# A hybrid decoder block on one core: GpSimd makes the RWKV stage's weight halves

## The chip, the cores and the metric

The kernel runs on one core of one Trainium2 chip. A core has five engines with a queue each, and each queue runs in order: TensorE (PE in the profile; its weight loads are listed apart as PEld), VectorE (DVE), ScalarE (ACT), GpSimd (POOL) and SyncE (SP), which here only issues DMAs. The metric is the device time of one execution in microseconds, lower is better; a time is given as the median of several runs.

## The reference

One decoder block over 512 tokens with a model width of 2048, batch 1, all in float32. What is computed, cut to its frame:

```python
c_act = silu(c)
mod = c_act @ w_ada + b_ada                     # six vectors: shift, scale, gate, twice
h = rmsnorm(x, norm1_g) * (1 + sc1) + sh1
p = h @ w_in                                    # 2048 -> 4384 columns
y_rwkv = rwkv7(p[..., :3360], ...)              # 16 heads of 64, state recurrence over 512 steps
y_pool = causal_pool(p[..., 3360:], ...)        # windows 2, 4, 8, 16
x = x + gt1 * (concat(y_rwkv, y_pool) @ w_out)
h = rmsnorm(x, norm2_g) * (1 + sc2) + sh2
x = x + gt2 * conv_ffn(h, w_up, conv_w, w_down) # 2048 -> 2 x 5632 -> 2048
out = rmsnorm(x, norm_f_g)
```

The projections need more precision than one pass of TensorE's rounded float type gives, so each is made of three products (below).

## The kernel before

**A projection.** Tokens lie along the free dimension (512 of them), features along the 128 partitions. Each activation tile is kept as two tiles, a rounded copy (hi) and the remainder (lo). Weights come in chunks of 128x512 floats (256 KB), that is four 128x128 blocks. `split_weights` loads a chunk into `wraw` (a DMA on SP's queue, four buffers), makes the rounded copy `whi` on ScalarE (L105, three buffers) and the remainder `wlo = wraw - whi` on VectorE (L107, three buffers). `mm3` then multiplies hi by hi (L111), hi by lo (L112) and lo by hi (L113) into one PSUM tile. One chunk feeds 12 matmuls, and `project` walks the chunks of one output tile. A `whi` buffer is free again when the last matmul on L112 of its chunk has run, a `wlo` buffer after the last on L113, and a `wraw` buffer when L107 has read it.

**The stages.** (1) Modulation vectors, the first norm, and the first eight tiles of the input projection (`pf`). (2) The RWKV stage, to which the change belongs: eight pairs of heads pass through `stage_a` (decay, keys, a small triangular solve on VectorE with trips through DRAM), `stage_b` (growing the inverse from 32 to 64 and 128 wide) and `stage_c` (four chunks of the recurrence, then a group norm). Among them stand the other 27 tiles of the input projection, made by `win_tile` into the PSUM tiles `mm` (two buffers): `win_pair` makes three for each of the pairs 1 to 7, and the last loop six more for the pooling groups. So 27 x 4 = 108 chunks are split in this stage. `ada_rest` (L334 and L336) works out the other modulation vectors on VectorE at the same time, 192 loads `war` and 192 dot products `jkr`. (3) The output projection, the second norm, the up projection with its convolution, and the down projection (`b` tiles), which fill the rest of the time.

**What sets the order.** The program is traced into a list, and the tile framework lays out ahead of time one fixed order for each engine: by priority, by what is ready in a plan that it makes with its own costs, and by which buffers are free. `hp()` puts the pairs' own work ahead of everything; the projection tiles and `ada_rest` fill in between. On the chip each engine follows its fixed order and waits at semaphores, so an instruction that waits holds up all that is behind it on its engine. Moving work to another engine makes the framework lay out all the orders anew.

**What else stands on the engines.** ScalarE has the activations of the pairs, with table loads, and the copies out of PSUM. VectorE has the masks, the triangular solve, the scans and `jkr`. GpSimd runs nothing but thirteen memsets, the last of them on L318 before the first pair. `project` and `split_weights` are also called in the stages (1) and (3).

Of the kernel before, what the change touches and what calls it, by code (L numbers as in the profile page):

```python
# [9 lines left out]
F32 = mybir.dt.float32  # L10
# [3 lines left out]
ALU = mybir.AluOpType  # L14
PSUM = bass.MemoryType.PSUM

P = 128
# [6 lines left out]
WC = 512  # L24
# [29 lines left out]
def block_kernel(ctx, tc, a, out, stop=None, dbg=None):  # L54
    nc = tc.nc
    V, S, G, PE = nc.vector, nc.scalar, nc.gpsimd, nc.tensor
# [41 lines left out]
    b1p = cp.tile([P, KT], F32, tag="b1p", name="b1p")  # L98
    V.tensor_scalar_add(b1p, cols("b_ada", 16, 32), 1.0)

    def split_weights(src):
        raw = wp.tile([P, WC], F32, tag="wraw", name="wraw", bufs=4)
        nc.sync.dma_start(raw, src)
        hi = wp.tile([P, WC], F32R, tag="whi", name="whi", bufs=3)
        S.copy(hi, raw)  # L105
        lo = wp.tile([P, WC], F32R, tag="wlo", name="wlo", bufs=3)
        V.tensor_tensor(lo, raw, hi[:, :].bitcast(F32), op=ALU.subtract)  # L107
        return hi, lo

    def mm3(ps, wh, wl, xh, xl, start, stop):  # L110
        PE.matmul(ps, wh, xh, start=start, stop=False)  # L111
        PE.matmul(ps, wh, xl, start=False, stop=False)  # L112
        PE.matmul(ps, wl, xh, start=False, stop=stop)  # L113

    def project(ps, src, acts, start=True, stop=True):

        n = len(acts)
        for k0 in range(0, n, WC // P):
            wh, wl = split_weights(src[:, k0 * P : k0 * P + WC])
            for kk in range(WC // P):  # L120
                k = k0 + kk
                sl = slice(kk * P, (kk + 1) * P)
                mm3(ps, wh[:, sl], wl[:, sl], *acts[k], start=start and k == 0, stop=stop and k == n - 1)

    def slots(k, tag="a"):
        return (actp.tile([P, T], F32R, tag=f"{tag}h{k}", name=f"{tag}h{k}"),
                actp.tile([P, T], F32R, tag=f"{tag}l{k}", name=f"{tag}l{k}"))
# [39 lines left out]
    if True:  # L167
# [27 lines left out]
        H = []  # L195
        for k in range(KT):
            for part in (1, 0):
                j = part * 16 + k
                wa = p0.tile([P, D], F32, tag="wa", name="wa", bufs=4)
                nc.sync.dma_start(wa, a["ada1"][j, :, :])  # L200
                jk = p0.tile([P, D], BF16, tag="jk", name="jk", bufs=1)
                V.scalar_tensor_tensor(jk, wa, 1.0, cb, op0=ALU.mult, op1=ALU.mult,
                                       accum_out=mod[:, j : j + 1])
            V.scalar_tensor_tensor(gsc1[:, k : k + 1], mod[:, 16 + k : 17 + k], b1p[:, k : k + 1],
                                   col("n1", k), op0=ALU.add, op1=ALU.mult)
            V.tensor_add(mod[:, k : k + 1], mod[:, k : k + 1], col("b_ada", k))
            h = p0.tile([P, T], F32, tag="h", name="h", bufs=2)
            hi, lo = slots(k)
            modulate(hi[:, :], lo[:, :], h, xs[k], rstd, gsc1[:, k : k + 1], mod[:, k : k + 1])
            H.append((hi, lo))  # L210
            for i0 in range(0, 8, WC // P):
                wh, wl = split_weights(a["win0"][k, :, i0 * P : i0 * P + WC])
                for ii in range(WC // P):
                    sl = slice(ii * P, (ii + 1) * P)
                    mm3(pf[i0 + ii], wh[:, sl], wl[:, sl], *H[k], start=k == 0, stop=k == KT - 1)
# [79 lines left out]
    def mmtile():  # L295
        return psa.tile([P, T], F32, tag="mm", name="mm", bufs=2)
# [9 lines left out]

    def win_tile(fi):
        ps = mmtile()
        project(ps, a["win1"][fi - 8, :, :], H)
        return ps  # L310

    sbd = [ra.tile([P, P], F32, tag=f"sbd{i}", name=f"sbd{i}") for i in range(2)]
# [278 lines left out]
    def win_pair(p):  # L591
        for i in range(3):
            ps = win_tile(8 + 3 * (p - 1) + i)
            t = ra.tile([P, T], F32, tag="spill", name="spill", bufs=2)
            shift(ps, 8 * i + p, t)
            d = tc.dram_tile([P, T], F32, name=f"sp{p}_{i}")
            nc.sync.dma_start(d, t)
            sp[p, i] = d
# [33 lines left out]
    for n, gi in enumerate((1, 2, 0)):  # L632
        upad = []
        for i in range(2):
            ps = win_tile(29 + 2 * n + i)
            u = ring16("upad")
            V.memset(u[:, 0:16], 0.0)
            S.copy(u[:, 16:], ps)
            upad.append(u)
        with hp():  # L640
            pool_group(gi)
# [17 lines left out]
    def bank():  # L659
        return psm.tile([P, T], F32, tag="b", name="b")  # L660
# [44 lines left out]
    def up_first(hf, k):  # L705
        hs = slice(hf * HT, (hf + 1) * HT)
        wh, wl = split_weights(a["wup0"][k, :, :])
        for i in range(4):
            sl = slice(i * P, (i + 1) * P)
            mm3(ups[i][:, hs], wh[:, sl], wl[:, sl], H2[k][0][:, hs], H2[k][1][:, hs], start=k == 0, stop=k == KT - 1)  # L710
# [4 lines left out]
    for k0 in range(0, KT, 4):  # L715
        for f in range(KT):
            project(pss[f], a["wout"][f, :, k0 * P : (k0 + 4) * P], mh[k0 : k0 + 4],
                    start=k0 == 0 and f % 2 == 0, stop=k0 == KT - 4 and f % 2 == 1)
        if k0 == 4:
            x2 = []  # L720
            for f in range(KT):
                t = rb.tile([P, T], F32, tag=f"x2_{f}", name=f"x2_{f}")
                nc.sync.dma_start(t, a["xT"][:, f, :])
                x2.append(t)
# [5 lines left out]
    for f in range(KT):  # L730
        if f == NORM_AT:
            dg = norm_rows(acc0)
        if f == NORM_AT + 1:
            rstd = norm_bcast(dg)
        if NORM_AT + 1 <= f < NORM_AT + 9:
            second_norm(0, rstd, 2 * (f - NORM_AT - 1))
            second_norm(0, rstd, 2 * (f - NORM_AT - 1) + 1)
        ps = bank()[:, 0:HT]
        project(ps, a["wout"][f, :, :], mh)
        acc1 = residual(1, f, ps, acc1)  # L740
# [49 lines left out]
    for gi, gn in enumerate(GROUPS):  # L790
# [17 lines left out]
        if gi < len(GROUPS) - 1:  # L808
            for f in range(KT):
                ps = bank()  # L810
# [131 lines left out]
```

## Time and profile before

| | us |
|---|---|
| median of 3 runs | 2465.12 (2463.72 to 2469.42) |
| the profiled execution's own time | 2465.06 |
| its span, from the first instruction to the last | 2463.3 |
| PE busy | 2355.7 (96%) |
| VectorE busy | 1450.8 (59%) |
| ScalarE busy | 912.6 (37%) |
| GpSimd busy | 2.7 |

The profile's times count from the start of the span. "Busy" for PE is the time covered by at least one matmul; matmuls overlap, so the time of one is read from the distance between two starts. In the table of waits a line says which instruction waited, for which, and how long its engine sat idle in total. In a group's line, the figure behind the bar's second stroke is the idle time of the engine just before these instructions, and what ended it. The RWKV stage lies between about 155 us and 800 us.

### The profile page before, as it was taken

How to read it: one execution, taken by the hardware profiler on the slowest of the kernel's cores; microseconds unless marked ns; L12 is line 12 of the kernel's file. 1: busy time of each engine (PE TensorE's matmuls, PEld its weight loads, DVE VectorE, ACT ScalarE, POOL GpSimd, SP SyncE). 2: the span in 40 equal slices, each digit the busy share in tenths (PEclk: the TensorE clock that was granted, in tenths of full speed). 3: DMA queues.
4: the chain of work that ended last, by engine and by line, in shares of the span. 5: the costliest groups of instructions: out<-in, count | busy, mean ns of one | idle time of the engine just before them, and what ended most of it. 6: DMA issues, size and time to landing. Idle time of an engine off the chain costs nothing.

```text
span 2463.3 us, 37835 instructions
## 1 busy us (share of the span) xinstructions
PE 2355.7 (96%) x14386; PEld 1907.4 (77%) x14386; DVE 1450.8 (59%) x2804; ACT 912.6 (37%) x1476; POOL 2.7 (0%) x13
## 2 busy tenths in 40 slices
PE   4889999999998999999999999999999999999997
PEld 3656666666665999887788888888888888888897
DVE  7987777787774477747634443444344433544467
ACT  3244443444334456533223322333233322323354
POOL 0000000000000000000000000000000000000000
PEclk9999999999999999999999999999999999999999
DMA  9965565566554755537532233223322232322255
GB/s 361 338 222 150 164 184 159 145 182 177 169 167 137 237 183 184 181 103 253 182 97 96 98 95 98 98 96 99 95 98 99 95 99 96 97 98 95 98 156 187
DMA packets 240232, 367.40 MB, mean 149 GB/s; under 512 B 75761, under 2 KB 81073, under 8 KB 235825
## 3 DMA queue, kind: packets, MB, share of 16 engines
q1 hardware_dynamic: 240050, 364.99, 46.8%
q8 instruction: 112, 1.84, 0.3%
q14 instruction: 70, 0.57, 0.1%
HBM read 348.90 MB, written 16.00 MB: 148 GB/s over the span
## 4 chain that ended last, share of the span: by engine, by line
PE 68%; DVE 3%; DMA 2%; ACT 1%; issue 1%; SPq 0%; DVEq 0%; ACTq 0%
PE b L113 21%; PE b L111 21%; PE b L112 21%; DMA slot<-ada 1%; DVE slot L774 1%; PE pa L283 1%; PE mm L111 1%; PE mm L112 1%; PE mm L113 1%; DVE wlo L107 0%; DMA wraw<-wup 0%; DMA war<-ada 0%; DMA mxl<-mixd 0%; DVE x L825 0%; PE pb L522 0%
## 5 line engine op out<-in xcount | busy, mean ns | idle before, releaser
L107 DVE TENSOR_TENSOR wlo<-wraw,whi 128x512 fp32r<-128x512 f32 x844 | 579.8, 689 | 694.6 <-ACT whi L105 681.9
L105 ACT CAST whi<-wraw 128x512 fp32r<-128x512 f32 x844 | 524.1, 622 | 1215.4 <-PE b L112 950.2
L113 PE MATMUL b<-hh,wlo 128*128 128x512 f32 (+1 forms) x1472 | 557.6, 381 | 9.7 <-DVE wlo L107 9.6
L111 PE MATMUL b<-hh,whi 128*128 128x512 f32 (+1 forms) x1472 | 559.2, 380 | 0.0
L112 PE MATMUL b<-hl,whi 128*128 128x512 f32 (+1 forms) x1472 | 558.6, 380 | 0.0
L111 PE MATMUL b<-ah,whi 128*128 128x256 f32 (+1 forms) x1344 | 442.2, 329 | 1.4 <-ACT mxp L286 0.9
L112 PE MATMUL b<-al,whi 128*128 128x256 f32 (+1 forms) x1344 | 441.3, 329 | 0.0
L113 PE MATMUL b<-ah,wlo 128*128 128x256 f32 (+1 forms) x1344 | 441.2, 329 | 0.0
L113 PEld LDWEIGHTS b<-hh,wlo 128*128 128x128 f32 x1472 | 275.6, 188 | 65.8 <-DVE wlo L107 13.3
L111 PEld LDWEIGHTS b<-hh,whi 128*128 128x128 f32 x1472 | 277.2, 188 | 53.1 <-ACT whi L105 0.5
L112 PEld LDWEIGHTS b<-hl,whi 128*128 128x128 f32 x1472 | 277.2, 188 | 52.0
L111 PEld LDWEIGHTS b<-ah,whi 128*128 128x128 f32 x1344 | 255.3, 190 | 26.9 <-ACT ah L131 2.4
L112 PEld LDWEIGHTS b<-al,whi 128*128 128x128 f32 x1344 | 255.5, 190 | 23.5 <-DVE al L132 1.0
L113 PEld LDWEIGHTS b<-ah,wlo 128*128 128x128 f32 x1344 | 255.4, 190 | 22.1 <-DVE wlo L107 0.2
L111 PE MATMUL mm<-ah,whi 128*128 128x512 f32 x432 | 179.1, 415 | 5.0 <-ACT upad L255 5.0
L112 PE MATMUL mm<-al,whi 128*128 128x512 f32 x432 | 178.4, 413 | 0.0
L113 PE MATMUL mm<-ah,wlo 128*128 128x512 f32 x432 | 177.3, 410 | 0.0
L336 DVE SCALAR_TENSOR_TENSOR jkr<-war,cq 128x512 bf16<-128x512 f32 x192 | 131.4, 684 | 20.9 <-DMA war<-ada 19.1
L812 DVE SCALAR_TENSOR_TENSOR x<-b,mod,x 128x512 f32<-128x512 f32 x80 | 59.7, 751 | 110.8 <-PE b L113 110.8
L111 PEld LDWEIGHTS mm<-ah,whi 128*128 128x128 f32 x432 | 82.0, 190 | 32.1 <-issue 10.2
L112 PEld LDWEIGHTS mm<-al,whi 128*128 128x128 f32 x432 | 82.1, 190 | 27.8 <-issue 12.7
L113 PEld LDWEIGHTS mm<-ah,wlo 128*128 128x128 f32 x432 | 82.1, 190 | 22.9 <-issue 6.9
(230 smaller groups left out, 2099.3 us busy)
## 6 DMA issues: line engine op xcount, KB each, us to landing
wraw<-wup SPq DMA_DIRECT2D x368, 256.0 KB, 3.0
wraw<-wdn SPq DMA_DIRECT2D x208, 256.0 KB, 2.7
war<-ada SPq DMA_DIRECT2D x192, 256.0 KB, 3.5
wraw<-win SPq DMA_DIRECT2D x140, 256.0 KB, 4.0
wa<-ada SPq DMA_DIRECT2D x32, 1024.0 KB, 7.1
wraw<-wout SPq DMA_DIRECT2D x128, 256.0 KB, 3.4
slot<-ada SPq DMA_DIRECT2D x64, 256.0 KB, 3.9
sp<-spill SPq DMA_DIRECT2D x21, 256.0 KB, 2.7
```

Source lines behind the costliest of these rows:

```text
L105: S.copy(hi, raw)
L107: V.tensor_tensor(lo, raw, hi[:, :].bitcast(F32), op=ALU.subtract)
L111: PE.matmul(ps, wh, xh, start=start, stop=False)
L112: PE.matmul(ps, wh, xl, start=False, stop=False)
L113: PE.matmul(ps, wl, xh, start=False, stop=stop)
L283: PE.matmul(ps, pw[:, i, d * P : (d + 1) * P], zs[i], start=i == 0, stop=i == 1)
L336: V.scalar_tensor_tensor(jk, wa, 1.0, cq[0], op0=ALU.mult, op1=ALU.mult, accum_out=modq[:, kq, j : j + 1])
L774: V.scalar_tensor_tensor(jk, wa, 1.0, cbs[kq], op0=ALU.mult, op1=ALU.mult, accum_out=modg[:, kq, j : j + 1])
L812: V.scalar_tensor_tensor(x2[f], ps, mod[:, 80 + f : 81 + f], x2[f], op0=ALU.mult, op1=ALU.add)
```

## The change

`split_weights` and `project` take a flag, and `win_tile` sets it: in the RWKV stage both halves of a chunk are made by GpSimd, the rounded copy with `tensor_copy` and the remainder with `tensor_tensor`. The DMA of the chunk, the buffers and the matmuls stay as they are in the code, and the other calls of `project` keep ScalarE and VectorE.

```diff
-    def split_weights(src):
+    def split_weights(src, pool=False):
         raw = wp.tile([P, WC], F32, tag="wraw", name="wraw", bufs=4)
         nc.sync.dma_start(raw, src)
         hi = wp.tile([P, WC], F32R, tag="whi", name="whi", bufs=3)
-        S.copy(hi, raw)
         lo = wp.tile([P, WC], F32R, tag="wlo", name="wlo", bufs=3)
-        V.tensor_tensor(lo, raw, hi[:, :].bitcast(F32), op=ALU.subtract)
+        if pool:
+            G.tensor_copy(hi, raw)
+            G.tensor_tensor(lo, raw, hi[:, :].bitcast(F32), op=ALU.subtract)
+        else:
+            S.copy(hi, raw)
+            V.tensor_tensor(lo, raw, hi[:, :].bitcast(F32), op=ALU.subtract)
         return hi, lo
...
-    def project(ps, src, acts, start=True, stop=True):
+    def project(ps, src, acts, start=True, stop=True, pool=False):
...
-            wh, wl = split_weights(src[:, k0 * P : k0 * P + WC])
+            wh, wl = split_weights(src[:, k0 * P : k0 * P + WC], pool)
...
     def win_tile(fi):
         ps = mmtile()
-        project(ps, a["win1"][fi - 8, :, :], H)
+        project(ps, a["win1"][fi - 8, :, :], H, pool=True)
         return ps
```

## The prediction

> **What bounds the kernel now.** I read the page's shares first, then the busy times of the RWKV stage alone, then who waited for whom in it.
>
> ```profile
> span 2463.3 us, 37835 instructions
> PE 2355.7 (96%) x14386; PEld 1907.4 (77%) x14386; DVE 1450.8 (59%) x2804; ACT 912.6 (37%) x1476; POOL 2.7 (0%) x13
> ```
>
> ```profile
> core 0: us, PE busy (x) PEld busy (x) DVE busy (x) ACT busy (x) POOL busy (x), PEclk, DMA share, GB/s
> 155.00:800.00 645.00, 613.55 (x5524) 421.40 (x5523) 469.30 (x1203) 274.44 (x422) 0.00 (x0) 0.98 0.56 165
> ```
>
> TensorE has matmuls in flight in 613.6 of the stage's 645 us. So 31.4 us of idle is all that a better flow on the other engines can win here, save the small stalls that overlapping matmuls cover. VectorE is busy 73% of the stage, ScalarE 43%, GpSimd not at all. The waits of PE in this stretch:
>
> ```profile
> PE pa L283 <- DMA pw<-poolw: 6.7, 1, 6.7
> PE mm L111 <- ACT upad L255: 5.0, 1, 5.0
> PE pa L402 <- DVE bt L394: 4.1, 2, 2.2
> PE ch L584 <- ACT rs L578: 3.5, 6, 0.9
> PE pb L455 <- DMA x<-dxz: 3.2, 3, 1.4
> PE pb L477 <- DVE xy L469: 3.0, 4, 1.9
> PE pb L465 <- issue: 1.1, 1, 1.1
> PE pa L360 <- DMA lw<-lora: 0.9, 2, 0.5
> PE pb L484 <- DVE Tm L479: 0.8, 1, 0.8
> PE pb L496 <- DVE x L488: 0.8, 2, 0.5
> PE ch L532 <- DVE L L524: 0.5, 2, 0.3
> PE pa L442 <- DVE nt L405: 0.4, 1, 0.4
> PE pb L501 <- ACT Tm L498: 0.2, 1, 0.2
> PE ch L576 <- ACT sqy L574: 0.2, 1, 0.2
> ```
>
> Neither `whi` nor `wlo` is among them: weights are not late today. The first two (11.7 us) stand at the ends of the stage: the PSUM of the `pf` tiles, which ScalarE must first copy out, and the last pooling group's weights. Of the rest, VectorE and ScalarE end 4.1 + 3.5 + 3.0 + 0.8 + 0.8 + 0.5 + 0.4 + 0.2 + 0.2 = 13.5 us, all work of the pairs.
>
> **What the change removes.** The groups of the stage by shape:
>
> ```profile
> L336 DVE SCALAR_TENSOR_TENSOR jkr<-war,cq 128x512 bf16<-128x512 f32 x192 | 131.4, 684 | 20.9 <-DMA war<-ada 19.1 <-DMA cq<-cact 0.4
> L107 DVE TENSOR_TENSOR wlo<-wraw,whi 128x512 fp32r<-128x512 f32 x110 | 75.3, 687 | 53.0 <-ACT whi L105 48.2 <-PE mm L113 2.3 <-PE mm L112 2.0
> L105 ACT CAST whi<-wraw 128x512 fp32r<-128x512 f32 x110 | 67.9, 619 | 153.3 <-PE mm L112 112.5 <-DMA wraw<-win 12.3 <-DVE jkr L336 6.4
> ```
>
> Of the 110 of each, 108 move (27 tiles of 4 chunks; the other two are neighbouring stages'). That takes 108 x 0.687 = 74 us off VectorE and 108 x 0.619 = 67 us off ScalarE. It also takes away waits that block a queue: ScalarE stood 153 us before the casts, mostly for a buffer that PE frees, with the pairs' work behind it, and VectorE 53 us for the cast. Where this reaches a pair, the chain of waits shows it:
>
> ```profile
> 677.98 0.62 ACT whi L105
> ...
> 678.61 1.28 ACT L578
> ```
>
> The cast is run just before the group norm's table load and logarithm on L578, for which L584 waits.
>
> What is it worth? None of the 13.5 us is a wait for the moved instructions themselves; it is a wait for pair work that shares an engine with them. The most it can give is the 13.5 us, the least nothing. The moved work with its waits is 75.3 + 53.0 of VectorE's 645 us and 67.9 + 153.3 of ScalarE's, 20% and 34%. If a stall shrank by the share of its engine, that would be about a quarter of 13.5; a cast that blocks just at the end of a chain, as above, counts for more. Between the two ends I take somewhat under half: 6 us.
>
> **What it adds.** No instruction of GpSimd in this trace reads anything. Its nearest rows are memsets:
>
> ```profile
> 0.73 0.53 POOL L72 MEMSET scanm<- 128x516 f32 x1 [0.29 <-POOLq L931]
> ...
> 149.93 0.96 POOL L316 MEMSET xy<- 128x1024 f32 x1
> ```
>
> That is about 0.5 us for one stream of 512 floats per partition. The copy has two streams: 0.5 us if they overlap, 1.0 if not. The subtraction has three: 0.5 to 1.6. So a chunk costs 1.0 to 2.6 us, against 0.62 + 0.69 = 1.31 on the two engines now. I take 2.1, the copy overlapped, the subtraction not, since the memsets show only that one stream is no slower than on VectorE. 108 x 2.1 = 227 us, 35% of the stage, on an engine that has nothing else; behind a GpSimd instruction that waits for a `whi` buffer there are only later chunks. [...]
>
> **Why that is hidden.** What PE needs is a chunk in time. The densest run of `mm` matmuls, and the casts in it:
>
> ```profile
> 684.70:703.70 19.00, 18.31 (x81) 14.83 (x79) 0.00 (x0) 1.16 (x2) 1.00 0.81 215
> ```
>
> ```profile
> 684.68 0.62 ACT L105 CAST whi<-wraw 128x512 fp32r<-128x512 f32 x1 [0.56 <-PE mm L112]
> 687.41 0.62 ACT L105 CAST whi<-wraw 128x512 fp32r<-128x512 f32 x1 [2.11 <-PE mm L112]
> ...
> 698.29 0.62 ACT L105 CAST whi<-wraw 128x512 fp32r<-128x512 f32 x1 [2.10 <-PE mm L112]
> 701.01 0.62 ACT L105 CAST whi<-wraw 128x512 fp32r<-128x512 f32 x1 [2.10 <-PE mm L112]
> ```
>
> One chunk each 2.72 us, for about seven chunks (81 of 84 matmuls), each cast waiting for the buffer that PE frees. Three chunks stand ready when a run begins. If GpSimd takes S per chunk, the seventh is ready about 2.3 + 4S after the start (the first release, then four chunks) and is needed by L113 at 6 x 2.72 + 0.45 = 16.8. So S may be 3.6 us before PE waits at all, and over the stage a chunk is used only each 645 / 108 = 6.0 us. At 2.1, and at 2.6, the late weights cost nothing. If that cover is gone (S over 3.6), it is the third rival.
>
> The queue in front moves little. SP issues `wraw` when the remainder has been read out of the old chunk:
>
> ```profile
> SPq L103 <- DVE wlo L107: 116.2, 40, 18.4
> ```
>
> Behind such a wait stand `war` loads, for which VectorE idled 19.1 us (row of L336). A release later by 2.1 - 1.31 = 0.8 us in 40 waits is 32 us of SP's time at most; in that proportion VectorE would lose 19.1 x 32 / 116 = 5 us more. That is a twelfth of what it is freed of, and I count it with the gain's discount. The buffers' number and the DMAs stay; the order of every engine is laid out anew, which can pack PE's queue better or worse by some microseconds either way.
>
> **The sum.** 2465.1 (the profiled execution, 0.06 us from the median of the runs) - 6 + 0 = 2459 us. A difference under 0.2%, 4.9 us, is about what a measurement of this kernel can't tell from none.
>
> **The rivals.**
>
> *First: no change, 2465.* The stage is 95% filled with matmuls; a wait that ends earlier on one engine may only be followed by the next (the DMA of `x`, 3.2 us, stands right behind the solve on VectorE). For it: the small size of all waits, and that no single one has the moved work as its releaser. Against it: the cast in the chain above.
>
> *Second: GpSimd holds VectorE up, slower, 2483.* While GpSimd reads its operands, a VectorE instruction with two operands in SBUF could have to wait for the whole of it, and the pairs' work on VectorE would come late. GpSimd is in the way for up to 227 us, and VectorE is freed of 75.3 + 53.0 = 128 us. The rival decides from the point where 128 / 227 = 56% of GpSimd's time falls on waiting VectorE instructions. At three quarters VectorE loses 170 - 128 = 42 us net, 5.3 in each of eight pairs. Projection matmuls that today run after the last pair can be pulled forward to fill PE's time:
>
> ```profile
> 759.00:787.00 28.00, 23.99 (x104) 1.00 0.54 168
> ```
>
> That is 24 us, 3.0 per pair, and leaves 2.3 x 8 = 18 us: 2483. For it: L336 (131 us) and the moved subtraction's neighbours read two SBUF tiles. Against it: the masks and copies of the recurrence read one of theirs from PSUM, and there PE takes few projection chunks.
>
> ```profile
> L524 DVE TENSOR_TENSOR L<-pb,masks 128x384 f32<-128x384 f32 x64 | 34.4, 554 | 15.7 <-PE pb L522 15.2
> L541 DVE COPY U<-ch 128x128 f32<-128x128 f32 x32 | 9.3, 290 | 21.9 <-PE ch L539 17.3 <-ACT R L535 3.6 <-ACT whi L105 0.6
> ```
>
> [...]
>
> *Third: chunks come late, 2476.* With 2.1 us and a VectorE instruction of 0.69 in front of each half, S is 3.5, just under 3.6. With 2.6 it is 4.0: (4.0 - 3.6) x 4 = 1.6 us in each of some seven dense runs, 11 us.
>
> *Fourth: a much better packing, 2448.* All 13.5 us go, and the small stalls that the matmuls' overlap hides, some 4 us more.
>
> **How the numbers follow.** The forecast has 0.40, with 2452 to 2464 as its own range; the first rival 0.27, the second 0.15, the third 0.10, the fourth 0.08. Below 2460.2 (faster) lie three quarters of the forecast and the fourth rival, 0.30 + 0.08, and 0.01 of the first: 0.39. Within 0.2% lie the forecast's rest and nearly all of the first: 0.10 + 0.25 = 0.35. Slower are the second, the third and 0.01 of the first: 0.26. The range, 2446 to 2484, holds the forecast, the first, third and fourth and the smaller half of the second; the least and greatest gain (0 and 13.5 with hidden stalls) and the dear end of a chunk (2.6 with VectorE in front) lie in it.
>
> **What would show it.** Right: GpSimd 200 to 240 us busy in the stage, a chunk near 2 us from start to start; VectorE and ScalarE some 70 us less busy each, and PE's waits for `bt`, `rs` and `xy` down by some 6 us; none on the new `whi` or `wlo`. The second rival: the mean of L336 or of the two-SBUF operations well over 0.69 us, or gaps before them that GpSimd ends, and more PE waits for `bt` and `xy`. The third: PE waits for `wlo` in dense runs. Wrong in any case: a shift outside 155 to 800 us, since nothing there is edited.

## The result, and the profile after

The changed kernel takes 2505.26 us (median of 4 runs, 2500.37 to 2512.29), the kernel before, run beside it, 2467.27 (2463.72 to 2470.67). The ratio is 1.0158, with a 95% interval of 1.0136 to 1.018: 38 us slower, where 2459 was forecast and the range ended at 2484. The profiled execution took 2505.43 us.

In the code after, the lines from `split_weights` on stand a few lower: L107 and L108 are GpSimd's copy and subtraction, L110 and L111 those that ScalarE and VectorE keep for the other stages; the matmuls of a chunk are L115 to L117, and everything later is 4 lower (L336 is L340, L586 is L590). In kernels of the experiments the lines move by a few more.

The page of the changed kernel, its span and shares, and then the RWKV stage alone (its end has moved from 800 to 838 us; columns as in the prediction):

```profile
span 2503.7 us, 37893 instructions
PE 2364.6 (94%) x14386; PEld 1912.3 (76%) x14386; DVE 1459.4 (58%) x2696; ACT 849.8 (34%) x1368; POOL 240.2 (10%) x229
```

```profile
155.00:838.00 683.00, 621.60 (x5530) 427.00 (x5529) 476.85 (x1098) 213.03 (x314) 234.46 (x214) 0.97 0.54 156
```

The stage is 38 us longer, so nearly the whole loss lies in it (the two profiled executions are 40.4 us apart). TensorE is idle for 683 - 621.6 = 61.4 us, twice the 31.4 of before, and covers 8 us more although it has the same matmuls. ScalarE lost 61 us of work, of the 67 forecast. VectorE did not get lighter: 108 subtractions are gone, and yet it is busy 476.9 us against 469.3. That is the line to stop at. The groups of the changed kernel on VectorE and GpSimd in the stage (busy us, mean ns of one, then idle before them), beside the one row of before that the prediction doesn't show:

```profile
L340 DVE SCALAR_TENSOR_TENSOR jkr<-war,cq 128x512 bf16<-128x512 f32 x192 | 146.4, 762 | 27.1 <-DMA war<-ada 23.7 <-DMA cq<-cact 1.6
L528 DVE TENSOR_TENSOR L<-pb,masks 128x384 f32<-128x384 f32 x64 | 34.4, 553 | 14.1 <-PE pb L526 13.2
L424 DVE TENSOR_TENSOR prod<-xyl,nl 64x14 f32<-64x14 f32 (+6 forms) x112 | 33.8, 302 | 1.5
L545 DVE COPY U<-ch 128x128 f32<-128x128 f32 x32 | 9.3, 289 | 25.4 <-PE ch L543 19.8 <-ACT R L539 4.3 <-PE pa L406 1.1
L108 POOL TENSOR_TENSOR wlo<-wraw,whi 128x512 fp32r<-128x512 f32 x107 | 155.7, 1455 | 25.2 <-PE mm L117 17.7
L107 POOL CAST whi<-wraw 128x512 fp32r<-128x512 f32 x107 | 79.7, 745 | 406.4 <-PE mm L116 402.4 <-PE pf L116 2.1 <-issue 1.9
```

```profile
L420 DVE TENSOR_TENSOR prod<-xyl,nl 64x14 f32<-64x14 f32 (+6 forms) x112 | 21.1, 189 | 1.3
```

A chunk costs GpSimd 0.75 + 1.46 = 2.2 us, as forecast, and GpSimd idles 400 us for buffers that TensorE frees. But `jkr` grew from 684 to 762 ns and the products of the triangular solve from 189 to 302 ns, while the mask (554, now 553) and the copy out of PSUM (290, now 289), which have an operand in PSUM, did not move. The timeline of one such instruction (start, length):

```profile
484.74 1.33 DVE L426 TENSOR_TENSOR xyl<-xyl,prod 64x56 f32<-64x56 f32 x1
```

```profile
484.72 1.28 POOL L108 TENSOR_TENSOR wlo<-wraw,whi 128x512 fp32r<-128x512 f32 x1
```

An instruction of 64 x 56 elements, 0.2 us by itself (mean 204 ns in the kernel before), starts 0.02 us behind a subtraction on GpSimd and ends 0.07 us after it: it was held for the whole of it. This is the mechanism of the prediction's second rival. The mask and the copy out of PSUM, with an operand in PSUM, were not held (553 and 289 ns). But two small copies within SBUF, with one input, did grow: the one of 128x4 from 166 to 449 ns, the one of 64x256 from 372 to 551. Why these two grew, no view here shows.

What TensorE waited for in the changed kernel (us in total, times, longest), and from the waits of all engines the one for the new halves:

```profile
PE pa L287 <- DMA pw<-poolw: 12.3, 2, 8.9
PE pa L364 <- DMA lw<-lora: 9.6, 5, 3.2
PE pb L459 <- DMA x<-dxz: 9.5, 6, 3.0
PE pa L406 <- DVE bt L398: 8.7, 2, 5.0
PE mm L115 <- DVE v L228: 6.1, 1, 6.1
...
PEld mm L117 <- POOL wlo L108: 2.3, 3, 0.8
```

The weights are not late (2.3 us, of TensorE's weight load alone). The pairs are: `bt` from 4.1 to 8.7, `x`, which comes back through DRAM behind the triangular solve, from 3.2 to 9.5, `lw` from 0.9 to 9.6. (In the same order without contention, an experiment below, `bt` waits 2.8, `x` 1.7 and `lw` 5.4 us.)

### The profile page after: what moved, and what is told of

It reads as the page before. It is cut to its first block, busy times and chain, and to the rows that moved or that the text cites. A ratio compares the mean times of both kernels' runs of the same rounds, so it can differ in the third digit from the quotient of the medians.

```text
span 2503.7 us, 37893 instructions
## 1 busy us (share of the span) xinstructions
PE 2364.6 (94%) x14386; PEld 1912.3 (76%) x14386; DVE 1459.4 (58%) x2696; ACT 849.8 (34%) x1368; POOL 240.2 (10%) x229
## 4 chain that ended last, share of the span: by engine, by line
PE 77%; DVE 10%; DMA 8%; issue 2%; ACT 1%; SPq 1%; POOL 1%; DVEq 0%; ACTq 0%; POOLq 0%
PE b L115 21%; PE b L117 21%; PE b L116 21%; DVE jk L206 3%; PE mm L116 2%; PE mm L117 2%; PE mm L115 2%; DMA war<-ada 2%; DVE jkr L340 1%; DMA x<-dxz 1%; PE pb L526 1%; PE pb L524 1%; PE pa L287 1%; DMA wraw<-wout 1%; PE pb L517 1%
## 5 line engine op out<-in xcount | busy, mean ns | idle before, releaser
L111 DVE TENSOR_TENSOR wlo<-wraw,whi 128x512 fp32r<-128x512 f32 x736 | 506.4, 690 | 645.7 <-ACT whi L110 638.8
L110 ACT CAST whi<-wraw 128x512 fp32r<-128x512 f32 x736 | 457.4, 622 | 1065.0 <-PE b L116 942.7
L117 PE MATMUL b<-hh,wlo 128*128 128x512 f32 (+1 forms) x1472 | 557.4, 381 | 8.3 <-DVE wlo L111 8.1
L115 PE MATMUL b<-hh,whi 128*128 128x512 f32 (+1 forms) x1472 | 559.1, 380 | 0.0
L115 PE MATMUL b<-ah,whi 128*128 128x256 f32 (+1 forms) x1344 | 442.6, 330 | 1.7 <-ACT whi L110 0.9
L117 PE MATMUL b<-ah,wlo 128*128 128x256 f32 (+1 forms) x1344 | 441.7, 329 | 0.9 <-DVE wlo L111 0.7
L117 PEld LDWEIGHTS b<-hh,wlo 128*128 128x128 f32 x1472 | 275.6, 188 | 64.0 <-DVE wlo L111 11.5
L115 PEld LDWEIGHTS b<-hh,whi 128*128 128x128 f32 x1472 | 277.2, 188 | 53.2 <-ACT whi L110 0.5
L115 PEld LDWEIGHTS b<-ah,whi 128*128 128x128 f32 x1344 | 255.3, 190 | 26.8 <-ACT ah L135 2.7
L117 PEld LDWEIGHTS b<-ah,wlo 128*128 128x128 f32 x1344 | 255.3, 190 | 24.1 <-DVE wlo L111 1.9
L115 PE MATMUL mm<-ah,whi 128*128 128x512 f32 x432 | 181.2, 419 | 6.1 <-DVE v L228 6.1
L117 PE MATMUL mm<-ah,wlo 128*128 128x512 f32 x432 | 179.2, 415 | 0.0
L340 DVE SCALAR_TENSOR_TENSOR jkr<-war,cq 128x512 bf16<-128x512 f32 x192 | 146.4, 762 | 27.1 <-DMA war<-ada 23.7
L108 POOL TENSOR_TENSOR wlo<-wraw,whi 128x512 fp32r<-128x512 f32 x108 | 157.2, 1456 | 25.3 <-PE mm L117 17.7
L107 POOL CAST whi<-wraw 128x512 fp32r<-128x512 f32 x108 | 80.8, 748 | 551.5 <-PE mm L116 402.4
L115 PEld LDWEIGHTS mm<-ah,whi 128*128 128x128 f32 x432 | 82.8, 192 | 31.3 <-issue 15.1
```

The costliest lines, as they stand in the source:

```text
L107: G.tensor_copy(hi, raw)
L108: G.tensor_tensor(lo, raw, hi[:, :].bitcast(F32), op=ALU.subtract)
L340: V.scalar_tensor_tensor(jk, wa, 1.0, cq[0], op0=ALU.mult, op1=ALU.mult, accum_out=modq[:, kq, j : j + 1])
```

## The experiments

Three theories stood at the start. A: contention, GpSimd holds up the pairs' work on VectorE. B: the orders, which the framework laid out anew, fit worse. C: the chunk's buffer is released later, so that the SP queue is late with the pairs' loads. Each run is compared with runs of the kernel before on the same chip (2464.3, 2467.1, 2466.4 and 2466.2 us in the four batches in which they ran).

### One part alone, orders left to the framework

GpSimd fills the halves with constants and reads two columns of the chunk, so nearly nothing is read:

```diff
-            G.tensor_copy(hi, raw)
-            G.tensor_tensor(lo, raw, hi[:, :].bitcast(F32), op=ALU.subtract)
+            G.tensor_copy(hi[:, 0:2], raw[:, 0:2])
+            G.memset(hi[:, 2:WC].bitcast(F32), 0.01)
+            G.memset(lo[:, 2:WC].bitcast(F32), 0.0001)
+            G.memset(lo[:, 2:WC].bitcast(F32), 0.0001)
+            G.tensor_copy(lo[:, 0:2], raw[:, 0:2])
```

> GpSimd fills both halves of a chunk with constants: one copy of 2 columns out of the loaded chunk and one memset of 510 for the rounded copy, two memsets of 510 and a last copy of 2 columns for the remainder. So the weights' values of the RWKV stage are left out; engines, dependences, the point at which the loaded chunk is released and about the time per chunk (some 1.8 us) stay, but nearly no read. Theory A (a GpSimd instruction that reads holds up VectorE's instructions with two SBUF operands, and that falls on the pairs' work): the 73 us by which 117 VectorE instructions are longer in the changed kernel vanish, and the time is 2455 to 2470. Theory B (the orders laid out anew with GpSimd in them are worse): still 2490 to 2515. Theory C (the chunk's buffer is released later, and SP's queue is late with the pairs' loads): still 2490 to 2515.

Only the copy on GpSimd (`V.tensor_tensor` stays), and only the subtraction (`S.copy` stays):

> Only the rounded copy goes to GpSimd, the remainder stays with VectorE. Theory A: GpSimd reads for 108 x 0.61 = 66 us instead of 206, so about a third of the 73 us, 24 us, and VectorE keeps the subtraction: 2472 to 2490. Theory B: anything up to the changed kernel's 2505. Theory C: the chunk is released by VectorE as before: 2460 to 2470.

> Only the remainder goes to GpSimd, the rounded copy stays with ScalarE. Theory A: two thirds of the 73 us, some 50: 2485 to 2500. Theory B: anything up to 2505. Theory C: the chunk is released by GpSimd as in the changed kernel: 2495 to 2510.

Nothing moved, and GpSimd makes both halves a second time:

```diff
+                sh = wp.tile([P, 256], F32R, tag="shi", name="shi", bufs=1)
+                G.tensor_copy(sh, raw[:, hs])
+                G.tensor_tensor(sh, raw[:, hs], sh[:, :].bitcast(F32), op=ALU.subtract)
```

> ScalarE and VectorE make both halves as before, and GpSimd makes them a second time into a scratch tile that nobody uses (in two halves of 256 columns, for space). Nothing is moved, only GpSimd's reading is added. Theory A: the 73 us come on top of a VectorE that keeps its subtractions: 2500 to 2530. Theory B: the orders are those of before, but for small shifts: 2460 to 2475. Theory C: the chunk is released by the last reader, GpSimd: 2490 to 2510.

| | us, median | ratio to before |
|---|---|---|
| filled with constants | 2488.24 | 1.011 (1.0087 to 1.0133) |
| copy alone | 2487.92 | 1.010 (1.0085 to 1.0115) |
| subtraction alone | 2513.35 | 1.0206 (1.0189 to 1.0223) |
| nothing moved, made twice | 2506.98 | 1.0173 (1.0145 to 1.0201) |

Every variant is slower, also the one filled with constants, which A had put at 2455 to 2470; it came out just under the 2490 to 2515 of B and C. So A isn't all of it. The copy alone and the halves made twice fell into A's ranges, the subtraction alone above all three. These runs can't be read further: each has orders of its own, and the parts don't add up.

### The orders held fixed

The next kernels take the orders out of the comparison. After the kernel is traced, each engine's instructions are chained in a given order, which fixes the order of issue and adds no wait:

```diff
-        block_kernel(tc, args, out)
+        block_kernel(tc, args, out), lay_order(tc)
...
+def lay_order(tc):
...
+    for e, s in ORDER.items():      # PE, ScalarE, VectorE, SP
...
+                tc.add_manual_dep(i, prev.name,
+                                  mybir.DependencyInfo(mybir.DependencyClass.NoSync, mybir.DependencyReason.DATA),
+                                  reason="order")
```

First the change itself, and the kernel that fills with constants, each in the order of the kernel before; then the kernel before in the order of the changed one; then the kernel before with a neutral edit, `ada_rest(min(24 * p, 192), min(24 * p + 24, 192))`, and orders left to the framework.

> The change, but TensorE, VectorE, ScalarE and the SP queue issue their instructions in exactly the order in which the kernel before issues them (the two instructions of a chunk are taken out of ScalarE's and VectorE's order and put on GpSimd). Theory B (of the 41 us that the change costs about 20 come from the orders that were laid out anew): this takes those 20 back and leaves the contention, 2482 to 2490 us. Theory A alone (all of it is GpSimd holding up VectorE) and theory C (the chunk's buffer is released later, so that the SP queue is late with the pairs' loads): nothing is taken back, 2500 to 2510.

> The kernel in which GpSimd fills the halves with constants and reads almost nothing (the projection's weights take no part in its result), now with the order of the kernel before on TensorE, VectorE, ScalarE and the SP queue. It has neither the contention nor the new orders. Theory B: 2455 to 2470 us. Theory C: it stays at what the filling kernel took without this, 2480 to 2490.

> The kernel before (ScalarE copies, VectorE subtracts, GpSimd does nothing in this stage), but TensorE, VectorE, ScalarE and the SP queue issue in the order that the changed kernel has; the copies and subtractions fall where the framework puts them between. Theory B: the new orders alone cost about 20 us, 2478 to 2492. Theories A and C: no cost, 2460 to 2470.

> The kernel before with one neutral difference: 24 instead of 28 of VectorE's weight reductions are issued after each pair, which changes no instruction but lets the framework lay all orders out anew. Theory B in its general form (the order of the kernel before happens to fit, and any new one is worse): 2475 to 2495 us. If the orders matter only through what the change does to them: 2460 to 2470.

Then the fourth corner, the filling kernel in the changed kernel's order:

> The kernel in which GpSimd fills the halves with constants (the projection's weights take no part in its result), with the orders of the changed kernel on TensorE, VectorE, ScalarE and the SP queue: the fourth corner beside the changed kernel (these orders, with contention, 2505), the one with the order of before and contention (2504) and the one with the order of before and none (2455). If the changed kernel's orders are bad in themselves (theory B), 2485 to 2500 us. If they are harmless and the whole loss is contention (theory A), 2452 to 2462.

| | order of before | order of the changed kernel |
|---|---|---|
| GpSimd fills, no contention | 2455.49, ratio 0.9952 (0.9937 to 0.9967) | 2469.46, ratio 1.0023 (1.0003 to 1.0043) |
| GpSimd reads (the change) | 2504.11, ratio 1.0143 (1.0112 to 1.0174) | 2505.26, ratio 1.0158 (1.0136 to 1.018) |
| nothing moved | the kernel before | 2515.17, ratio 1.0205 (1.0183 to 1.0227) |

The neutral edit took 2481.18 us, ratio 1.0054 (1.0035 to 1.0072).

The table can be read in two directions. Down the left column, with every order that of before: moving the work gains 11.6 us, and contention then costs 48.6. Along the other way, in the changed kernel's order: the gain of 11.6, then 14.6 for the order, then 35.0 for contention, together 38. The two costs overlap: with contention, taking the order back saves nothing (2504 against 2505), which is where B's expectation for that run failed. The filling kernel in the changed kernel's order, 2469, lies between the expectations of A and B: that order costs, but less than B had put. With nothing moved it goes with 48 us, more than B's 2478 to 2492. There the framework placed the copies and subtractions, so this is not the price of the order alone, and no run separates the two.

"No contention" is meant nearly: beside GpSimd that fills, the two small copies within SBUF are longer as well (486 and 714 ns), 5 us in all.

As a cause by itself C falls: the filling takes GpSimd 204.4 / 107 = 1.9 us for a chunk (row below), over the 1.31 of before, so a chunk's buffer is released late there too, and in the order of before that kernel is the fastest of the table. SP's waits for the remainder in it are as long as before (116.2):

```profile
SPq L103 <- POOL wlo L111: 115.7, 48, 18.4
```

Where GpSimd reads, SP does wait longer for it: 181.6 us in the changed kernel, against 152.8 when GpSimd fills in that order. So part of what contention costs can come through SP's queue; no run separates that part.

B stands as a cost of its own: 14.6 us here, 14 for a neutral edit, 28 for the copy alone (23.6 above the kernel before in its own order, 4.2 below it in that of before, under the next heading), 36 for the filling kernel (23.9 above in its own order, 11.6 below).

### Where the contention costs

The two kernels of the left column issue the same instructions in the same order on four engines. The stage of each, filling and then reading:

```profile
155.00:790.00 635.00, 611.18 (x5524) 420.25 (x5523) 412.55 (x1096) 213.60 (x316) 204.44 (x530) 0.99 0.57 168
```

```profile
155.00:842.00 687.00, 638.41 (x5530) 437.04 (x5528) 487.88 (x1099) 214.69 (x316) 246.17 (x214) 0.94 0.52 155
```

VectorE is busy 75.3 us longer for the same work. Half of it, 37 us, falls on the two lines of the triangular solve, 14 us on `jkr`. The solve, filling and then reading:

```profile
L427 DVE TENSOR_TENSOR prod<-xyl,nl 64x14 f32<-64x14 f32 (+6 forms) x112 | 21.9, 195 | 1.8
L429 DVE TENSOR_TENSOR xyl<-xyl,prod 64x14 f32<-64x14 f32 (+6 forms) x112 | 21.2, 189 | 1.6
```

```profile
L426 DVE TENSOR_TENSOR xyl<-xyl,prod 64x14 f32<-64x14 f32 (+6 forms) x112 | 41.7, 373 | 1.6
L424 DVE TENSOR_TENSOR prod<-xyl,nl 64x14 f32<-64x14 f32 (+6 forms) x112 | 38.5, 344 | 1.8
```

The stage is 52 us longer: TensorE idles 48.6 us against 23.8, and is busy 638.4 against 611.2 for the same matmuls, at a granted clock of 0.94 against 0.99. TensorE's waits, filling and then reading:

```profile
PE pb L462 <- DMA x<-dxz: 3.7, 2, 1.9
...
PE pb L484 <- DVE xy L476: 1.0, 3, 0.5
...
PE ch L591 <- ACT rs L585: 0.8, 2, 0.5
```

```profile
PE pb L459 <- DMA x<-dxz: 16.3, 5, 5.2
...
PE pa L406 <- DVE bt L398: 5.0, 2, 3.3
```

Without contention the waits that the prediction set out to shorten did go or shrink: `bt` from 4.1 to nothing, `rs` from 3.5 to 0.8, `xy` from 3.0 to 1.0. In all, what VectorE and ScalarE end of the pairs' waits fell from 13.5 to 4.8 us. With it, the round trip of `x` behind the solve goes from 3.7 to 16.3.

The remaining runs test contention by itself, its parts and its grain. Nothing moved, the halves made a second time, order of before:

> The kernel before in its own order with nothing moved: ScalarE copies and VectorE subtracts as before, and GpSimd makes both halves a second time into a scratch tile that nobody reads. Contention alone. Theory A: about 49 us above the kernel before, less what is not moved anyway, 2495 to 2515. If the contention hurts only beside the moved work's new place: 2465 to 2480.

2510.86 us, ratio 1.018 (1.0141 to 1.0219). Contention alone, on the kernel before, costs 44 us; A's number. (A chunk's buffer is released after GpSimd's second reading here, so a late release is in it too.)

The change in the order of before, with one constant in the place of all the projection's weights:

> The change in the order of the kernel before, with every element of the projection's weights set to one constant, which GpSimd reads, rounds and subtracts as it does the true ones. If the 49 us between the reading and the filling kernel are contention: 2492 to 2512 us, as with the true weights. If the constant weights themselves made the filling kernel fast (TensorE at a higher clock): 2455 to 2470.

2497.67 us (2493.58 to 2504.41), ratio 1.0127 (1.0103 to 1.015), beside 2504.11 (2491.92 to 2508.44) with the true weights. The medians differ by 6 us, with intervals that overlap, so the data explain at most a few of the 49 us; the filling kernels' gain of 11.6 may hold a few as well. The granted clock was 0.98 with constant weights and 0.977 with the true ones.

The copy alone, and the two reliefs without contention (the half named is filled with a constant, the other one made as before), all in the order of before:

> GpSimd makes only the rounded copy, VectorE goes on subtracting, and all four engines keep the order of the kernel before. In its own order this kernel's VectorE instructions were longer by 19 us together, against 74 us where GpSimd also subtracts. Theory A with a price that follows the lengthening (49 us of time for 76 us of VectorE's waits, 0.64 each): 2460 to 2470 us. If the price follows GpSimd's busy time instead (81 of 204 us undisturbed): 2472 to 2482. If the hand-over from GpSimd to VectorE costs by itself: over 2482.

> All in the order of the kernel before: GpSimd fills the rounded half with a constant and reads almost nothing, VectorE subtracts as before, ScalarE makes no copies in this stage (the projection's weights take no full part in the result). ScalarE's relief alone, without contention. If the gain of 12 us comes from the casts that stood in ScalarE's queue: 2452 to 2460 us, and what the reading copy adds to it (2462) is contention, 2 to 10 us. If it comes from VectorE: 2463 to 2468.

> All in the order of the kernel before: ScalarE copies as before, GpSimd fills the remainder with a constant and reads almost nothing, VectorE makes no subtraction in this stage. VectorE's relief alone, without contention. If the gain of 12 us comes from VectorE: 2452 to 2460 us. If it comes from ScalarE: 2463 to 2468.

| order of before | us, median | ratio to before |
|---|---|---|
| rounded half filled by GpSimd | 2455.91 | 0.9961 (0.9951 to 0.9971) |
| rounded half copied by GpSimd | 2462.18 | 0.9979 (0.9969 to 0.999) |
| remainder filled by GpSimd | 2460.03 | 0.9982 (0.9972 to 0.9992) |

ScalarE's relief is worth about 10 us, VectorE's 6 (neither as exclusive as the expectations had it), both together 11.6. The copy gives back some 6 us of its 10: GpSimd's reading of one operand disturbs far less than the subtraction. So GpSimd copying and VectorE subtracting, in the order of before, computes the whole result and is 0.2% faster than the kernel before, 1.8% faster than the changed one. The gain is there only while the order is held: in its own order the same kernel is 1.0% slower than before.

Last, GpSimd's subtraction in four pieces of 128 columns, order of before:

```diff
-            G.tensor_tensor(lo, raw, hi[:, :].bitcast(F32), op=ALU.subtract)
+            for j in range(4):
+                js = slice(j * P, j * P + P)
+                G.tensor_tensor(lo[:, js], raw[:, js], hi[:, js].bitcast(F32), op=ALU.subtract)
```

> The change in the order of the kernel before, with GpSimd's subtraction cut into four pieces of 128 columns. If a VectorE instruction waits only until the GpSimd instruction that it meets has ended, its wait shrinks with the piece: VectorE's waits fall from 76 us to 35 to 50 and the time to 2475 to 2490 us. If it loses in proportion to GpSimd's busy time however that is cut: 2500 to 2515.

2496.42 us, ratio 1.0115 (1.0098 to 1.0132), between the two expectations. Its stage, and those of the copy alone and of the kernel that makes the halves twice:

```profile
155.00:832.00 677.00, 626.08 (x5528) 429.05 (x5526) 457.03 (x1100) 214.37 (x315) 328.46 (x536) 0.96 0.54 159
```

```profile
155.00:796.00 641.00, 611.90 (x5523) 419.50 (x5521) 484.41 (x1203) 212.80 (x315) 86.04 (x106) 0.99 0.57 166
```

```profile
155.00:830.00 675.00, 621.22 (x5525) 424.45 (x5523) 531.04 (x1206) 275.06 (x422) 335.98 (x427) 0.97 0.55 160
```

VectorE's surplus falls from 75.3 to 457.0 - 412.6 = 44.5 us, so a wait does shrink with the piece, but GpSimd is now in the way for 328 us, and the time falls by 8 us only. Over the pairs of kernels that differ mainly in reading, a microsecond of VectorE's surplus cost, between the profiled executions, 51.0 / 75.3 = 0.68 us (change), 33.4 / (531.0 - 469.3) = 0.54 (nothing moved) and 40.9 / 44.5 = 0.92 (pieces). (The medians give 0.65 and 0.72 for the first two; the kernel that makes the halves twice was profiled in the fastest of its four executions.) It is no fixed price, and the solve's share of the surplus doesn't explain it: 37 of 75 us, 18.7 of 61.7, 23.5 of 44.5, and for the copy alone, at a price of 0.53, 8.7 of 13.1. In pieces a chunk takes GpSimd 3.0 us, and SP waits 176.9 us for the remainder, so a later release may be in that price. That the cost comes mostly through the pairs' chain is read from the waits; no run kept the contention off the pairs and left it on `jkr`.

## Why the prediction was wrong

**What held.** The bound (TensorE, with 31 us of idle to win), the cost of a chunk (2.1 forecast, 2.2 measured; 1.9 undisturbed, so that the 2.2 holds GpSimd's own waits and its nearness to 2.1 is in part luck), the cover for the weights (no wait over 1 us for them), the place of the shift (38 of 40 us within the stage), and the mechanism of the gain: without contention, in the same order, the waits for `bt`, `rs` and `xy` went or shrank.

**The gain, mis-sized low.** 6 us was "somewhat under half" of 13.5 us of waits. Measured alone it is 11.6 by the medians (8 to 16 by the interval), and 7.7 between the profiled executions, where TensorE idles 7.6 us less. Of the 13.5 us, 8.7 went, more than the quarter that the engines' loads suggested. Why it is more was not tested.

**The step that failed first: the + 0 of the sum, and the second rival's balance behind it.** The sum counts nothing for what GpSimd's reading does to VectorE, and leaves it to the second rival. That rival's mechanism is the one that came, with the signs that the prediction gave for it: `jkr` at 762 ns, the two-operand operations longer, more waits for `bt`. Its chance was 0.15 and its time 2483, where 2505 was measured, because its balance was wrong. It said GpSimd must hold VectorE for 128 us, 56% of its own time, before the change loses, because VectorE was freed of 75.3 + 53.0 us. VectorE was held for 75 us in the order of before, 31% of GpSimd's 246, and contention cost 49 us all the same. The balance set time freed against time lost on one engine, as if they were the same kind of time. Measured, the 74 us that VectorE was freed of were worth 6 us (the remainder filled by GpSimd), the 75 us of holding 49. The subtractions that left were filler, which waits for its own operands and can be placed anywhere; half of what was held is the solve, whose 28 short operations stand one behind the other on the way to `x`. Freed filler didn't pay for a longer chain. In the kernel where nothing was moved, 62 us of holding cost 33 us in the profiled execution, 44 by the medians. How the 49 us divide between the chain itself and a later release of the chunks' buffers stays open.

**The evidence against that rival was read too kindly.** That the recurrence's masks read PSUM was right (554 and 553 ns), but the solve, `bt`, `kt` and `ar` read two SBUF tiles, and the prediction quoted no row of theirs.

**The price of late pairs.** The rival let 24 us of projection matmuls be pulled forward from behind the last pair. They were not. The product that ends a pair, before and after (shortest, median, longest in ns, then the first and last start):

```profile
L586 DVE TENSOR_TENSOR rs<-rs,ch x8: 669/687/690, 292.1 to 758.4; 128x512 f32<-128x512 f32 x8
```

```profile
L590 DVE TENSOR_TENSOR rs<-rs,ch x8: 669/673/689, 300.3 to 790.6; 128x512 f32<-128x512 f32 x8
```

The last one starts 32 us later, and from there to the end of the stage it is 838 - 790.6 = 47 us, where it was 800 - 758.4 = 42. In that stretch TensorE runs 132 matmuls of `mm` (30.4 us), where it ran 106 (24.6 us). Pauses have also cost beyond themselves, since behind some of them the granted clock fell to 0.50 (below).

**The orders, "some microseconds either way".** Alone they cost 14.6 us, and a neutral edit as much. The kernel before was not an average of the orders that the framework can lay out: all the new ones that ran without contention or with little of it (after the change, 14.6; the filling kernel, 36; the copy alone, 28; a neutral edit, 14) were slower. The price belongs in a forecast with its own sign and size, even if here, beside the contention, it showed little: the change takes 2504 and 2505 us in the two orders.

**SP's release.** Counted at up to 5 us, it is not seen without contention: with the slow chunk the kernel is then faster than before. With contention, in the changed kernel, SP waits 65 us longer, where the prediction allowed at most 32; 37 of the 65 come with the order alone (152.8 against 116.2). (Its 5 us are not a twelfth of the 74 us that VectorE is freed of, but about a fourteenth; nothing hangs on it.)

## What to carry to other kernels

Before work with SBUF operands goes to GpSimd, list the VectorE instructions with two SBUF operands that run at the same time, and ask whether they stand in a chain that the bottleneck waits for; here 75 us of holding cost 49 us, although VectorE was freed of 74. One operand read on GpSimd (a copy) was cheap here, some 6 us; with the subtraction, which reads two, it was 49. When an edit lets a planner lay out all orders anew, compare at a fixed order as well, or a good and a bad reason can't be told apart.

## What the runs showed of the hardware

**The clock can stay low long after a short pause.** In the change with the order of before, TensorE's granted clock (the third figure from the right) over steps of 3 us:

```profile
258.00:261.00 3.00, 3.00 (x38) 2.02 (x36) 0.36 (x1) 0.00 (x0) 0.09 (x1) 1.00 0.68 220
261.00:264.00 3.00, 1.40 (x4) 0.58 (x3) 2.44 (x6) 0.00 (x0) 2.23 (x2) 0.87 1.06 246
264.00:267.00 3.00, 3.00 (x43) 2.92 (x44) 0.60 (x2) 0.00 (x0) 0.17 (x1) 0.50 0.87 272
...
285.00:288.00 3.00, 3.00 (x18) 1.83 (x17) 1.82 (x5) 0.00 (x0) 0.00 (x0) 0.50 0.67 246
288.00:291.00 3.00, 3.00 (x25) 2.24 (x23) 0.12 (x2) 1.04 (x3) 0.00 (x0) 0.58 0.34 88
291.00:294.00 3.00, 2.96 (x33) 1.91 (x32) 1.79 (x5) 0.28 (x1) 0.00 (x0) 1.00 0.00 0
```

After 1.6 us of idle (0.5 and 1.1 us, for the two halves of a chunk) it ran at 0.50 for some 27 us (about 263 to 290), with matmuls in flight nearly throughout. It is the longest such stretch: the mean clock was 0.73 over 250 to 300 us, 0.88 or more over every other 50 us of the stage, and the stretch behind 613 us lasted some 10 us. Not every pause was followed by one: with 1.35 us of idle between 243 and 246 us the clock stayed at 1.00. Why the return took 27 us here stays open. So pauses here cost beyond themselves: 25 us more idle in the stage came with 27 us more of busy time for the same matmuls (in the changed kernel in its own order, 30 and 8). This execution was the slowest of its four (2491.92 to 2508.44), and by an estimate, half of 27 us, this one stretch cost some 13 us of it.

**GpSimd's times**, from the change in the order of before (shortest, median, longest in ns):

```profile
L107 POOL CAST whi<-wraw x108: 601/612/2671, 146.1 to 818.5; 128x512 fp32r<-128x512 f32 x108
```

```profile
L108 POOL TENSOR_TENSOR wlo<-wraw,whi x108: 1260/1292/3993, 147.2 to 819.4; 128x512 fp32r<-128x512 f32 x108
```

Undisturbed, the copy is 0.61 us and the subtraction 1.29. GpSimd waits for VectorE as well: in the changed kernel a subtraction took 3.16 us from 610.40 on, while VectorE ran `bt`, `k` and `jkr`, each with two inputs in SBUF, one behind the other in 0.68, 0.74 and 0.68 us, none of them held.
